# A two-layer DiT block on one core: four modulation groups summed row block by row block on VectorE, ScalarE and GpSimd instead of TensorE, layer 1's in layer 0's dense part

## The chip, the cores and the metric

The kernel runs on one core of a Trainium2 chip. Its engines are TensorE (PE; its weight loads are the rows PEld), VectorE (DVE), ScalarE (ACT), GpSimd (POOL) and SyncE (SP), which issues most of the transfers. The metric is the device time of one execution in microseconds (us), as the median of several.

## The reference

Two token streams, x and ctx, of 256 tokens by 1024 channels pass two layers; of layer 1 only x is needed. Cut to what matters:

```
mod_x = silu(c) @ w_mod[l] + b_mod[l]            # 1024 x 6144, six vectors
sh1, sc1, g1, sh2, sc2, g2 = split(mod_x, 6)     # and the same for ctx from c_ctx
p = modulate(rmsnorm(x, norm1_g[l]), sh1, sc1) @ w_in[l]
q, k, v, conv, pool, gate = split_in(p)
y = sigmoid(ga) * (attn @ w_attn_o) + sigmoid(gb) * (conv_module @ w_conv_o) + sigmoid(gc) * (pooled @ w_pool_o)
x = x + g1 * (y @ w_out[l])
x = x + g2 * expert_choice_ffn(modulate(rmsnorm(x, norm2_g[l]), sh2, sc2), ...)   # 16 experts, 12 MB each
```

So the modulation is a product of one or two vectors with a 1024 x 6144 matrix per layer. The kernel deals with it in three groups of 2048 columns: group 0 holds shift and scale of the first norm, group 1 the gate g1 and the shift of the second norm, group 2 its scale and the gate g2.

## The kernel before

**Units.** A layer's dense part works through products of the normalised tokens (512 columns in layer 0, 256 in layer 1) with weight blocks of 128 columns. Each such `unit` loads half of a 1 MB block (`w`, a ring of five buffers of 1 MB, filled by SP's queue in program order), splits it (`split`: ScalarE copies the high part, L227; VectorE or GpSimd, by the table `LOW`, subtracts for the low part, L228) and runs three passes of eight matmuls (`mm3`: L483, L484, and L486 with the low part). The units in order are q, k and v, the convolution's, the pooling's, and three merges (0, 2, 1) with eight gate units each. Each unit of a merge has an own output product beside it and ends on VectorE with `m` (L743, merge 0) or `th` (L746, the others), which in the latter case GpSimd adds to m (L748).

**Attention and convolution.** After a q or k product ScalarE reads it out (`raw`, L512, and `qx`, L529), GpSimd applies the rotary tables in two operations (L517 and L518), and ScalarE writes `QC` and `QS` (L535). v is turned by PE and copied to `vt` by VectorE (L556). The depthwise convolution of 31 taps runs on VectorE as multiply-adds (L465); they are issued a few at a time among the units (the table `TAPS`).

**Modulation.** `mod_group` forms one group on PE: for each of 8 blocks of 128 rows (a k-step), four matmuls (L244) whose stationary operand is silu(c), of 32 columns, and whose moving operand is the weight block of 128x2048 in four strips of 512. Bias, transposes and copies follow. It is a Python generator, and `pump_mod` advances it by one k-step per unit (every second unit in layer 1). Layer 0 so runs its own groups 1 and 2 and layer 1's group 0; layer 1 runs its groups 1 and 2. Layer 0's group 0 is formed ahead of all in another function, which stays.

**Order.** The program is put in order on each engine by a scheduler, with the program's order as priority; splits have a higher one (`SPLIT_PRIO`). `prefetch` asks for the first expert weights (`we`), in layer 0 two of them after attention. After the dense part come the product with w_out (L859), the routing, and 16 experts whose weights stream in blocks of 1 MB.

Of the kernel before, what the change touches and what calls it, by code (L numbers as in the profile page):

```python
# [10 lines left out]
F32 = mybir.dt.float32  # L11
F32R = mybir.dt.float32r
BF16 = mybir.dt.bfloat16
# [16 lines left out]
MOD_EVERY = (1, 2)  # L30
MOD_AHEAD = 1
# [3 lines left out]
KC_ID, KC_PERM, KC_IOTA, KC_SCOL, KC_EDGE, KV_C, KV_VEC, KV_END = 0, 128, 256, 288, 289, 353, 369, 433  # L35


def const_tables():

    f = np.float32  # L40
    kc = np.zeros((128, KV_C), f)
    p = np.arange(128)
    kc[:, KC_ID:KC_ID + 128] = np.eye(128, dtype=f)
    kc[p ^ 16, KC_PERM + p] = 1.0
    kc[:, KC_IOTA:KC_IOTA + 32] = np.arange(1, 33)
    kc[:, KC_SCOL] = p % 32 + 1
# [21 lines left out]
    return kc, b16.astype(mybir.dt.np(BF16)), rope.reshape(128, 2 * SEQ)  # L68


def laid_out(a):

    kc, b16, rope = const_tables()
    L = DEPTH
# [12 lines left out]
    cols = np.concatenate([dwc, snk], axis=2)  # L87
# [3 lines left out]
    bm[0, 0] = np.repeat(first, 32, axis=0)  # L91
    w_in = a["w_in"].reshape(L, 8, 128, 21, 256).transpose(0, 3, 2, 1, 4).copy()
# [3 lines left out]
    def blocks(w, order):  # L96
# [10 lines left out]
        ("w_mod0", w_mod0.reshape(2, 4, 128, 2048)), ("w_mod", a["w_mod"]), ("b_mod", bm),  # L107
# [13 lines left out]
def dit_block(ctx: ExitStack, tc: tile.TileContext, out, kcv, kb16, rope_in, tok, cols, w_mod0, w_mod,  # L121
# [53 lines left out]
    bt = P0.tile([128, 768], BF16, name="bt")  # L175
    identb, maskb = bt[:, 0:128], bt[:, 128:384].rearrange("p (a b) -> p a b", a=2)
    ucat = bt[:, 384:768].rearrange("p (a b) -> p a b", a=3)
# [4 lines left out]
    cst = P0.tile([128, 8, 2, 16], F32, name="cst")  # L182
# [18 lines left out]
    for l in range(DEPTH):  # L201
# [14 lines left out]
        nsplit, nunit, tail = [0], [0], [False]  # L216
# [14 lines left out]
        def mod_group(ll, g):  # L231
            ps = bank("md")

            def mload(k):
                return load(w_mod[ll, k * 128:(k + 1) * 128, g * 2048:(g + 1) * 2048], "p n -> p n")

            w = mload(0)
            for k in range(8):
                if k == 6:
                    bias = t2("modb", 512)  # L240
                    nc.scalar.dma_start(bias, b_mod[ll, g])
                wn = mload(k + 1) if k < 7 else None
# [18 lines left out]
            ptv = pt.rearrange("p (b j s m) -> p s j b m", b=4, j=4, s=2)
            for s in range(2):
                nc.vector.tensor_copy(modT[ll][:, g, s, :].rearrange("p (j b) -> p j b", j=4),
                                      ptv[:, s, :, :, 0])
            if g == 0:
                for s in range(2):
# [3 lines left out]
            if g == 2:  # L270
                for s in range(2):
# [15 lines left out]
        def layer_vectors():
            nc.scalar.dma_start(dws, cols[l])
# [3 lines left out]
        dws = DR.tile([128, 4 * CK + NH], F32, name="dw")  # L292
        dw, sink = dws[:, :4 * CK], dws[:, 4 * CK:]
# [126 lines left out]
        if l == 0:  # L420
# [5 lines left out]
            nc.scalar.dma_start(bt, kb16)  # L426
# [10 lines left out]
        wr = P0.tile([128, 8, 32], F32, tag="wr", name="wr")  # L437
        nc.scalar.dma_start(wr.rearrange("p k e -> p (k e)"), w_router[l])
        nc.sync.dma_start(rope.rearrange("p a t -> p (a t)"), rope_in)
        bg = deque([[(0, 1), (0, 2), (1, 0)], [(1, 1), (1, 2)]][l])  # L440
        cur_mod = [None]

        def pump_mod(n=1):

            while n > 0:
                if cur_mod[0] is None:
                    if not bg:
                        return
                    cur_mod[0] = mod_group(*bg.popleft())
                if next(cur_mod[0], "end") == "end":  # L450
                    cur_mod[0] = None
                else:
                    n -= 1
# [15 lines left out]
        if last:  # L469
            pump_mod(MOD_AHEAD)  # L470
# [17 lines left out]
        def unit(src, n, view="p (k n) -> p k n", eng="v", **kw):  # L488
# [21 lines left out]
        def roped(dst, ps):  # L510
# [3 lines left out]
            nc.tensor.matmul(pr[:, 0:256], kc[:, KC_PERM:KC_PERM + 128], raw, start=True, stop=True)  # L514
# [168 lines left out]
        prefetch(4 if last else 2)  # L683
# [6 lines left out]
        for u in range(2):  # L690
            wz = win(OP + 256 * u)
            for v in range(2):
# [19 lines left out]
                ed = kc[:, KC_EDGE + 16 * g:KC_EDGE + 16 * g + 16]  # L712
# [39 lines left out]

        merge(0, w_attn_o, br)
# [54 lines left out]
        pump_mod(100)  # L808
# [375 lines left out]
```

## Time and profile before

| | |
|---|---|
| median of 3 runs | 1722.48 us (1722.29 to 1725.2) |
| the profiled execution | 1721.98 us, span 1720.2 us |
| PE busy | 1515.4 us, 88% of the span |
| VectorE, ScalarE, GpSimd busy | 672.5, 407.7, 229.7 us |
| moved by DMA | 530 MB, mean 308 GB/s |

The rows below come from the profiled execution. Times are from the start of its span. A busy share over the whole span mixes dense parts and expert parts.

### The profile page before, as it was taken

The numbers are of one execution on the slowest core, as the hardware profiler recorded it, in microseconds if no ns is written. First come the engines' busy times: TensorE is split into PE (matmuls) and PEld (weight loads), VectorE is DVE, ScalarE is ACT, GpSimd is POOL, SyncE is SP. The second block draws the span as 40 slices with busy tenths as digits, with TensorE's granted clock in tenths as the row PEclk, the third lists the DMA queues.
The fourth block names the chain that finished last, engine by engine and source line by source line (L and its number), as shares of the span: only waits on it lengthen the run. The fifth ranks groups of instructions, "written<-read, shape, count | busy, mean of one in ns | idle before, by whom it ended". The sixth has DMA issues, their size and how long they took to land. (4 is left out here: it accounts for less than half of the span.)

```text
span 1720.2 us, 19498 instructions
## 1 busy us (share of the span) xinstructions
PE 1515.4 (88%) x7788; PEld 822.1 (48%) x7788; DVE 672.5 (39%) x1137; ACT 407.7 (24%) x760; POOL 229.7 (13%) x234
## 2 busy tenths in 40 slices
PE   6999989999999999999999899999979766666675
PEld 2665667888654433333333367789844111111111
DVE  3568993352552221221211368975532110111111
ACT  3455312232432100100000257334421000000001
POOL 0300520154640000000000020225100000000000
PEclk9999999999999999999999999999989898988989
DMA  9733445244536999999999864566789999999996
GB/s 398 276 122 129 147 147 202 78 152 165 220 147 267 421 421 421 421 420 421 421 422 420 334 240 178 201 232 226 278 334 420 421 421 421 421 421 421 422 421 272
DMA packets 78171, 530.04 MB, mean 308 GB/s; under 512 B 8449, under 2 KB 9217, under 8 KB 15106
## 3 DMA queue, kind: packets, MB, share of 16 engines
q1 hardware_dynamic: 76208, 526.12, 76.5%
q10 hardware_dynamic: 1874, 2.70, 0.5%
q8 instruction: 61, 1.00, 0.2%
q14 instruction: 28, 0.23, 0.0%
HBM read 527.73 MB, written 1.05 MB: 307 GB/s over the span
## 5 line engine op out<-in xcount | busy, mean ns | idle before, releaser
L1065 PE MATMUL mm<-we,xeT 128*64 128x512 f32 (+1 forms) x2048 | 414.4, 620 | 78.6 <-DMA we<-in_w_e_up_dram 59.7
L1065 PEld LDWEIGHTS mm<-we,xeT 128*64 128x64 f32 (+1 forms) x2048 | 125.0, 125 | 361.7 <-issue 191.5
L483 PE MATMUL mm<-hh,ws 128*128 128x512 f32 (+1 forms) x672 | 223.0, 350 | 0.2
L484 PE MATMUL mm<-hl,ws 128*128 128x512 f32 (+1 forms) x672 | 219.2, 345 | 0.8 <-DVE hl L418 0.8
L227 ACT ACTIVATE ws<-w 128x1024 fp32r<-128x1024 f32 x132 | 139.2, 1057 | 300.3 <-PE mm L486 196.9
L1072 DVE TENSOR_TENSOR hm<-si,mm 64x512 f32<-64x512 f32 x48 | 33.1, 690 | 419.7 <-ACT si L1070 283.1
L1070 ACT ACTIVATE si<-mm 64x512 f32<-64x512 f32 x48 | 28.4, 591 | 693.8 <-PE mm L1065 693.8
L465 DVE SCALAR_TENSOR_TENSOR acc<-up,dw,acc 128x512 f32<-128x512 f32 (+1 forms) x240 | 156.6, 692 | 1.1
L228 DVE TENSOR_TENSOR ws<-w,ws 128x1024 fp32r<-128x1024 f32 x94 | 124.7, 1329 | 67.5 <-ACT ws L227 67.4
L483 PEld LDWEIGHTS mm<-hh,ws 128*128 128x128 f32 x672 | 128.1, 191 | 28.8 <-issue 11.8
L484 PEld LDWEIGHTS mm<-hl,ws 128*128 128x128 f32 x672 | 128.1, 191 | 19.6 <-issue 3.5
L1088 PE MATMUL mm<-we,hT 128*64 128x512 f32 x512 | 126.1, 625 | 8.4 <-ACT hT L1083 8.4
L486 PE MATMUL mm<-hh,ws 128*128 128x512 f32 (+1 forms) x672 | 132.6, 339 | 0.7 <-DVE ws L228 0.6
L228 POOL TENSOR_TENSOR ws<-w,ws 128x1024 fp32r<-128x1024 f32 x38 | 95.4, 2517 | 213.9 <-ACT ws L227 213.9
L486 PEld LDWEIGHTS mm<-hh,ws 128*128 128x128 f32 x672 | 107.2, 189 | 15.3 <-DVE ws L228 1.3
L1030 POOL COPY sel<-kc 48x128 f32<-48x128 f32 (+1 forms) x16 | 4.6, 287 | 806.4 <-DVE hm L1072 434.6
L1093 PE MATMUL mm<-we,hT 128*32 128x512 f32 x512 | 83.4, 764 | 15.0 <-DMA we<-in_w_e_down_dram 11.2
L1100 DVE TENSOR_TENSOR Y<-mm,G 32x512 f32<-32x512 f32 x64 | 44.0, 687 | 126.4 <-PE mm L1088 125.7
L1088 PEld LDWEIGHTS mm<-we,hT 128*64 128x64 f32 x512 | 38.3, 143 | 86.3 <-issue 72.4
L1110 PE MATMUL ax<-Y,sg 128*128 128x512 f32 x128 | 62.5, 636 | 8.0 <-DVE Y L1103 6.4
L1080 PE MATMUL ax<-kc,hm 64*128 64x64 f32 x192 | 32.4, 291 | 31.1 <-DVE hm L1072 30.3
L1103 DVE TENSOR_TENSOR Y<-mm,G 64x512 f32<-64x512 f32 x32 | 22.0, 689 | 95.2 <-PE mm L1093 94.8
(254 smaller groups left out, 1624.3 us busy)
## 6 DMA issues: line engine op xcount, KB each, us to landing
we<-in_w_e_gate_dram SPq DMA_DIRECT2D x128, 1024.0 KB, 19.8
we<-in_w_e_up_dram SPq DMA_DIRECT2D x128, 1024.0 KB, 19.8
we<-in_w_e_down_dram SPq DMA_DIRECT2D x120, 1024.0 KB, 19.8
w<-in_w_mod_dram SPq DMA_DIRECT2D x44, 1024.0 KB, 6.3
w<-in_w_in_dram SPq DMA_DIRECT2D x42, 1024.0 KB, 4.9
w<-in_w_out_dram SPq DMA_DIRECT2D x12, 1024.0 KB, 4.8
we<-in_w_e_down_dram SPq DMA_DIRECT2D x16, 512.0 KB, 14.8
wm<-in_w_mod_dram SPq DMA_DIRECT2D x4, 1024.0 KB, 18.1
```

The costliest lines, as they stand in the source:

```text
L227: nc.scalar.activation(h, src, AF.Copy)
L228: (nc.gpsimd if eng == "p" else nc.vector).tensor_sub(lw, src, h.bitcast(F32))
L465: nc.vector.scalar_tensor_tensor(acc[:, ch], up[:, ch, :, k:k + 256], dw[:, 4 * k + ch:4 * k + ch + 1], acc[:, ch], op0=ALU.mult, op1=ALU.add)
L483: nc.tensor.matmul(ps, wh[:, k, :], ah[:, k, :n], start=k == 0, stop=False)
L484: nc.tensor.matmul(ps, wh[:, k, :], al[:, k, :n], start=False, stop=False)
L486: nc.tensor.matmul(ps, wl[:, k, :], ah[:, k, :n], start=False, stop=k == nk - 1)
L1065: nc.tensor.matmul(o, xeT[k // 4][:, k % 4, e, :], w[:, kk, 512 * f:512 * f + 512], start=k == 0, stop=k == 7)
L1072: nc.vector.tensor_mul(hm[0:64, :], si[0:64, :], pgu[f][64:128, :])
L1088: nc.tensor.matmul(pd[64 * h:64 * h + 64, :], hT[:, 64 * k:64 * k + 64], rhs, start=k == 0, stop=k == 7)
L1093: nc.tensor.matmul(pd[o:o + 32, :], hT[:, c0:c0 + 32], rhs, start=k < 2, stop=k >= 6)
L1100: nc.vector.tensor_mul(Y[b0:b0 + 32, s, cols], pd[rw, :], G2[l][rw, :])
L1110: nc.tensor.matmul(po, sgs[s][:, t * 128:(t + 1) * 128], Y[:, s, cols], start=True, stop=True)
```

## The change

A generator `vmod` takes the place of `mod_group`. It has three forms.

- Layer 1's group 0 stays on PE, with 256-column strips.
- Layer 0's groups 1 and 2 are summed on VectorE: each block of 128 rows and 1024 columns is multiplied by that block's column of silu(c) and added to an accumulator `macc` of 128x1024 per stream (L279 for the first block, L281 for the others; 64 in all).
- Layer 1's groups 1 and 2, of stream x only, are summed by two engines: ScalarE multiplies a block in place (L275, 32 in all) and GpSimd adds it to the accumulator (L277, 28).

For each half of a group one product of `macc` with a matrix of ones (L295, eight matmuls of 256 columns) then sums over the 128 partitions. There are two generators, `vgen`: PE's and VectorE's groups in the first, ScalarE's and GpSimd's in the second. `pump_mod` advances both after every unit, by the counts of `VSTEPS` for the stage. All of it, layer 1's w_mod loads too, is in layer 0's dense part; layer 1 keeps a selection and one matmul (`gate2`). The accumulators use the buffers in which the first two experts' weights were prefetched, so layer 0's prefetch moves behind merge 1. w_mod is laid out in blocks of 1 MB, the router's weights are loaded later, and some constant tables move to other buffers.

```diff
-MOD_EVERY = (1, 2)
-MOD_AHEAD = 1
+VSTEPS = dict(qkv=(1, 1), conv=(1, 1), pool=(2, 1), merge=(3, 1))
...
-        def mod_group(ll, g):
...
-                for j in range(4):
-                    nc.tensor.matmul(ps[32 * j:32 * j + 32, :],
-                                     cst[:, k].rearrange("p s m -> p (s m)"),
-                                     w[:, j * 512:(j + 1) * 512], start=k == 0, stop=k == 7)
-                w = wn
+        def vmod(ll, gs, tag):
+            pairs = [(gs[0], 0), (gs[0], 1)] if len(gs) == 1 else [(g, 0) for g in gs]
+            def mload(i):
+                hf, k2 = divmod(i, 4)
+                ws = [load(w_mod[ll, g, hf, k2], "p (k n) -> p k n", k=2) for g in gs]
+                return ws if len(gs) == 2 else ws * 2
...
+                for k2 in range(4):
+                    i = 4 * hf + k2
+                    wn = mload(i + 1) if i < 7 else None
+                    for kk in range(2):
+                        k = 2 * k2 + kk
...
+                        for q, (g, s) in enumerate(pairs):
+                            cs = csil[:, 8 * s + k:8 * s + k + 1]
+                            wk = w[q][:, kk]
+                            if len(gs) == 2:
+                                nc.scalar.activation(wk if k else ac[:, q], wk, AF.Copy, scale=cs)
+                                if k:
+                                    nc.gpsimd.tensor_add(ac[:, q], ac[:, q], wk)
+                            elif k == 0:
+                                nc.vector.tensor_scalar(ac[:, q], wk, cs, None, op0=ALU.mult)
+                            else:
+                                nc.vector.scalar_tensor_tensor(ac[:, q], wk, cs, ac[:, q],
+                                                               op0=ALU.mult, op1=ALU.add)
+                            yield
...
+                if tag is not None:
+                    for _ in range(3):
+                        yield
+                    ps = bank("md")
+                    for q in range(2):
+                        for j in range(4):
+                            nc.tensor.matmul(ps[32 * j:32 * j + 32, 0:256], ones[:, q],
+                                             ac[:, q, 256 * j:256 * j + 256], start=q == 0, stop=q == 1)
+                nc.vector.tensor_add(mr[:, 256 * hf:256 * hf + 256], ps[:, 0:256], bias)
...
-        bg = deque([[(0, 1), (0, 2), (1, 0)], [(1, 1), (1, 2)]][l])
...
+        vgen = [[], []]
+        if not last:
+            def on_dve():
+                yield from vmod(1, (0,), None)
+                yield from vmod(0, (1,), "e0")
+                yield from vmod(0, (2,), "e0")
+            vgen = [on_dve(), vmod(1, (1, 2), "e1")]
...
+            for g, n in zip(vgen, VSTEPS[vphase[0]] if every is None else (every, every)):
+                for _ in range(n):
+                    next(g, None)
...
-        prefetch(4 if last else 2)
+        if last:
+            prefetch(4)
...
         merge(1, w_conv_o, brc)
-        pump_mod(100)
+        pump_mod(1000)
+        if not last:
+            prefetch(2)
```

ScalarE's order before, from the read-out of the first q product on (names with buffer numbers; in the changed kernel L512, L529, L535 and L227 are L562, L579, L585 and L234):

```order
L512 ACTIVATE raw_353<-mm_318 128x256
L529 ACTIVATE qx_352<-mm_318 128x256
L535 ACTIVATE QC_313<-qx_352 64x256 x2
L535 ACTIVATE QS_310<-qx_352 64x256
L227 ACTIVATE ws_424<-w_422 128x1024
L227 ACTIVATE ws_476<-w_422 128x1024
L535 ACTIVATE QS_310<-qx_352 64x256
L512 ACTIVATE raw_405<-mm_373 128x256
L529 ACTIVATE qx_404<-mm_373 128x256
L535 ACTIVATE QC_313<-qx_404 64x256 x2
```

The same place after, from the read-out of the second q product on:

```order
L562 ACTIVATE raw_431<-mm_394 128x256
L275 ACTIVATE w_365<-w_365,csil_68 128x1024
L579 ACTIVATE qx_430<-mm_394 128x256
L275 ACTIVATE w_368<-w_368,csil_68 128x1024
L585 ACTIVATE QS_315<-qx_430 64x256
L585 ACTIVATE QC_318<-qx_430 64x256
L585 ACTIVATE QS_315<-qx_430 64x256
L585 ACTIVATE QC_318<-qx_430 64x256
L275 ACTIVATE w_368<-w_368,csil_68 128x1024
L275 ACTIVATE w_370<-w_370,csil_68 128x1024 x2
L234 ACTIVATE ws_450<-w_448 128x1024
L234 ACTIVATE ws_508<-w_448 128x1024
```

Seven L275 now stand behind the first read-out and ahead of the split of the next weight, L234 on w_448; five of them are in the rows above, and two stand before the rows' first, among the operations on the first product.

GpSimd's order there before, over the first q products:

```order
L517 TENSOR_TENSOR qx<-raw,rope 128x256
L518 TENSOR_TENSOR qx<-qx,rot 128x256
L517 TENSOR_TENSOR qx<-raw,rope 128x256
L518 TENSOR_TENSOR qx<-qx,rot 128x256
L517 TENSOR_TENSOR qx<-raw,rope 128x256
```

And after (L517 and L518 are now L567 and L568):

```order
L567 TENSOR_TENSOR qx<-raw,rope 128x256
L277 TENSOR_TENSOR macc<-macc,w 128x1024
L568 TENSOR_TENSOR qx<-qx,rot 128x256
L567 TENSOR_TENSOR qx<-raw,rope 128x256
L568 TENSOR_TENSOR qx<-qx,rot 128x256
L277 TENSOR_TENSOR macc<-macc,w 128x1024 x5
```

One L277 stands between the two rotary operations of the first product, and five stand ahead of the third product's.

VectorE's order in merge 0 before, from the third m on (L465 is the convolution, L228 the low part of a split):

```order
L743 SCALAR_TENSOR_TENSOR m<-th,mm 128x512
L465 SCALAR_TENSOR_TENSOR acc<-up,dw,acc 128x512 x4
L228 TENSOR_TENSOR ws<-w,ws 128x1024
L743 SCALAR_TENSOR_TENSOR m<-th,mm 128x512
L228 TENSOR_TENSOR ws<-w,ws 128x1024 x2
L743 SCALAR_TENSOR_TENSOR m<-th,mm 128x512
L228 TENSOR_TENSOR ws<-w,ws 128x1024
L743 SCALAR_TENSOR_TENSOR m<-th,mm 128x512
L228 TENSOR_TENSOR ws<-w,ws 128x1024 x2
L743 SCALAR_TENSOR_TENSOR m<-th,mm 128x512
```

And after (L801 is m, L519 the convolution, L235 the low part, L297 the addition of a bias), up to the fifth m:

```order
L235 TENSOR_TENSOR ws<-w,ws 128x1024
L297 TENSOR_TENSOR GM<-md,modb 128x256
L279 TENSOR_SCALAR macc<-w,csil 128x1024
L801 SCALAR_TENSOR_TENSOR m<-th,mm 128x512
L279 TENSOR_SCALAR macc<-w,csil 128x1024
L281 SCALAR_TENSOR_TENSOR macc<-w,csil,macc 128x1024 x6
L801 SCALAR_TENSOR_TENSOR m<-th,mm 128x512
L519 SCALAR_TENSOR_TENSOR acc<-up,dw,acc 128x512
L235 TENSOR_TENSOR ws<-w,ws 128x1024 x2
L281 SCALAR_TENSOR_TENSOR macc<-w,csil,macc 128x1024 x4
L235 TENSOR_TENSOR ws<-w,ws 128x1024
L801 SCALAR_TENSOR_TENSOR m<-th,mm 128x512
```

The multiply-adds of layer 0's group 1 (L279, L281) stand between the m, where before only low parts and a few convolution taps stood; taps from before the first m have moved in between too.

GpSimd's order there before, from the last pooling sums to merge 2's additions to m:

```order
L708 TENSOR_TENSOR zs<-zs 128x2x257
L715 TENSOR_TENSOR zs<-zs,kc 128x8 x4
L748 TENSOR_TENSOR m<-m,th 128x512 x5
L777 TENSOR_SCALAR rl<-bmv 128x1
L778 TENSOR_TENSOR rl<-rl,nhalf 128x1
```

And after (L806 is the addition to m):

```order
L773 TENSOR_TENSOR zs<-zs,dw 128x8 x4
L277 TENSOR_TENSOR macc<-macc,w 128x1024 x10
L806 TENSOR_TENSOR m<-m,th 128x512
L277 TENSOR_TENSOR macc<-macc,w 128x1024 x2
L806 TENSOR_TENSOR m<-m,th 128x512
L277 TENSOR_TENSOR macc<-macc,w 128x1024 x2
L806 TENSOR_TENSOR m<-m,th 128x512 x3
```

Ten L277 stand between the last pooling operation and merge 2's first addition, and four more among the next two.

## Rows read from the trace of the kernel before

**Rows 1.** The page: busy times; DMA share in 40 slices of 43 us, tenths.

```profile
PE 1515.4 (88%) x7788; PEld 822.1 (48%) x7788; DVE 672.5 (39%) x1137; ACT 407.7 (24%) x760; POOL 229.7 (13%) x234
...
DMA  9733445244536999999999864566789999999996
```

**Rows 2.** Windows: layer 0's dense part; stretch, length, busy us (instructions) by engine.

```profile
47.00:82.00 35.00, 34.75 (x167) 23.66 (x165) 20.40 (x29) 17.49 (x35) 13.23 (x12) 1.00 0.71 261
...
82.00:235.70 153.70, 145.78 (x662) 93.26 (x661) 130.11 (x228) 67.37 (x155) 37.13 (x42) 0.98 0.37 128
...
235.70:297.70 62.00, 62.00 (x292) 44.67 (x292) 33.59 (x43) 14.11 (x18) 0.00 (x0) 1.00 0.60 211
...
297.70:362.30 64.60, 64.60 (x297) 52.61 (x296) 34.74 (x46) 20.11 (x26) 15.99 (x18) 1.00 0.25 88
...
362.30:437.70 75.40, 75.40 (x331) 61.77 (x330) 20.49 (x20) 23.35 (x32) 36.51 (x22) 1.00 0.46 169
```

**Rows 3.** VectorE's timeline in merges 0 and 1: start us, us, instruction, [idle before <-releaser].

```profile
278.88 0.69 DVE L743 SCALAR_TENSOR_TENSOR m<-th,mm 128x512 f32<-128x512 f32 x1 [1.71 <-PE mm L486]
...
288.26 0.69 DVE L743 SCALAR_TENSOR_TENSOR m<-th,mm 128x512 f32<-128x512 f32 x1 [1.70 <-PE mm L486]
...
378.65 0.69 DVE L746 SCALAR_TENSOR_TENSOR th<-th,mm 128x512 f32<-128x512 f32 x1 [1.75 <-issue]
...
386.81 0.69 DVE L746 SCALAR_TENSOR_TENSOR th<-th,mm 128x512 f32<-128x512 f32 x1 [7.47 <-PE mm L486]
```

**Rows 4.** By form (ns min/median/max, first and last start); one row of VectorE's timeline.

```profile
L465 DVE SCALAR_TENSOR_TENSOR acc<-up,dw,acc x240: 454/736/2891, 102.2 to 1145.5; 128x512 f32<-128x512 f32 x60, 128x256 f32<-128x256 f32 x60
...
L227 ACT ACTIVATE ws<-w x132: 1037/1059/1087, 22.9 to 1244.9; 128x1024 fp32r<-128x1024 f32 x132
...
L228 POOL TENSOR_TENSOR ws<-w,ws x38: 2375/2404/3146, 63.4 to 1176.8; 128x1024 fp32r<-128x1024 f32 x38
...
183.42 6.70 DVE L465 SCALAR_TENSOR_TENSOR acc<-up,dw,acc 128x512 f32<-128x512 f32 x10
```

**Rows 5.** Timeline of VectorE and GpSimd in two stretches, both busy.

```profile
438.24 11.39 DVE L814 TENSOR_TENSOR ml<-m,mh 128x512 fp32r<-128x512 f32 x6
...
440.04 8.45 POOL L228 TENSOR_TENSOR ws<-w,ws 128x1024 fp32r<-128x1024 f32 x3
...
192.48 6.37 DVE L465 SCALAR_TENSOR_TENSOR acc<-up,dw,acc 128x512 f32<-128x512 f32 x5
...
194.04 2.76 POOL L228 TENSOR_TENSOR ws<-w,ws 128x1024 fp32r<-128x1024 f32 x1 [9.77 <-ACT ws L227]
```

**Rows 6.** Timeline after the first q product, and the start of attention.

```profile
47.61 0.38 ACT L512 ACTIVATE raw<-mm 128x256 f32<-128x256 f32 x1 [5.14 <-PE mm L486]
...
49.35 0.91 POOL L518 TENSOR_TENSOR qx<-qx,rot 128x256 f32<-128x256 f32 x1 [0.55 <-DVE rot L516]
...
50.61 1.99 ACT L227 ACTIVATE ws<-w 128x1024 fp32r<-128x1024 f32 x2
...
51.70 0.19 PEld L483 LDWEIGHTS mm<-hh,ws 128*128 128x128 f32 x1 [1.03 <-ACT ws L227]
...
82.23 0.69 DVE L556 COPY vt<-ax 128x512 f32<-128x512 f32 x1 [0.24 <-PE ax L555]
```

**Rows 7.** Layer 1: first and last of seven L244 pieces of the chain; windows.

```profile
1036.79 0.99 PE md L244 x6
...
1175.54 1.00 PE md L244 x8
...
980.00:1000.00 20.00, 17.21 (x93) 10.04 (x92) 16.83 (x31) 13.25 (x31) 3.51 (x5) 1.00 0.45 172
...
1100.00:1120.00 20.00, 17.40 (x140) 15.10 (x138) 19.91 (x43) 5.84 (x8) 4.60 (x7) 1.00 0.70 257
```

**Rows 8.** The expert parts: last pieces of the chain; a window of layer 0.

```profile
1655.13 19.85 DMA we<-in_w_e_down_dram
...
550.00:600.00 50.00, 49.31 (x260) 22.44 (x258) 12.00 (x21) 7.61 (x15) 0.58 (x2) 1.00 1.01 416
```

More of the change, by code (lines that the diff above doesn't have):

```diff
@@ L67, in const_tables @@
     b16[:, 640:768] = 1.0
-    return kc, b16.astype(mybir.dt.np(BF16)), rope.reshape(128, 2 * SEQ)
+    return kc, dk, b16.astype(mybir.dt.np(BF16)), rope.reshape(128, 2 * SEQ)
 def laid_out(a):
-    kc, b16, rope = const_tables()
+    kc, dk, b16, rope = const_tables()
     L = DEPTH
@@ L91, in laid_out @@
     bm[0, 0] = np.repeat(first, 32, axis=0)
+    bm[1, 1] = np.where(np.arange(128)[:, None] % 32 < 16, bm[1, 1], bm[1, 2])
+    w_mod = a["w_mod"].reshape(L, 4, 2, 128, 3, 4, 2, 256).transpose(0, 4, 6, 1, 3, 2, 5, 7)
     w_in = a["w_in"].reshape(L, 8, 128, 21, 256).transpose(0, 3, 2, 1, 4).copy()
@@ L174, in dit_block @@
         nc.sync.dma_start(XS[s].rearrange("p t d -> p (t d)"), tok[s])
-    bt = P0.tile([128, 768], BF16, name="bt")
-    identb, maskb = bt[:, 0:128], bt[:, 128:384].rearrange("p (a b) -> p a b", a=2)
-    ucat = bt[:, 384:768].rearrange("p (a b) -> p a b", a=3)
+    bt = P0.tile([128, 384], BF16, name="bt")
+    ucat = bt.rearrange("p (a b) -> p a b", a=3)
+    ones = P0.tile([128, 2, 32], F32, name="ones")
+    for i in range(2):
+        for j in range(2):
+            nc.vector.memset(ones[:, i, 16 * j:16 * j + 16], float(i == j))
     nc.scalar.activation(csil, ccol, AF.Tanh, scale=0.5)
@@ L265, in mod_group @@
-            if g == 0:
-                for s in range(2):
+                                      ptv[:, q, :, :, 0])
+                if g == 0:
                     nc.vector.scalar_tensor_tensor(
@@ L269, in mod_group @@
                         vec[:, VN1 + 8 * ll:VN1 + 8 * ll + 8], op0=ALU.add, op1=ALU.mult)
-            if g == 2:
-                for s in range(2):
+                if g == 2:
                     nc.vector.scalar_tensor_tensor(
@@ L436, in dit_block, with pump_mod @@
             qw = [qload(0)]
-        wr = P0.tile([128, 8, 32], F32, tag="wr", name="wr")
-        nc.scalar.dma_start(wr.rearrange("p k e -> p (k e)"), w_router[l])
+            layer_tables()
         nc.sync.dma_start(rope.rearrange("p a t -> p (a t)"), rope_in)
-        bg = deque([[(0, 1), (0, 2), (1, 0)], [(1, 1), (1, 2)]][l])
[L441 to L453, printed above, removed]
+        vgen = [[], []]
[5 more added lines that the diff above has]
+            vgen = [on_dve(), vmod(1, (1, 2), "e1")]
+        vgen = [iter(v) for v in vgen]
+        vphase = ["qkv"]
+        def pump_mod(every=None):
+            for g, n in zip(vgen, VSTEPS[vphase[0]] if every is None else (every, every)):
+                for _ in range(n):
+                    next(g, None)
         taps = deque()
@@ L513, in roped @@
             pr = bank("ax")
-            nc.tensor.matmul(pr[:, 0:256], kc[:, KC_PERM:KC_PERM + 128], raw, start=True, stop=True)
+            nc.tensor.matmul(pr[:, 0:256], perm, raw, start=True, stop=True)
             rot = t2("rot", 256)
@@ L681, in dit_block @@
             pass
-        prefetch(4 if last else 2)
+        if last:
+            prefetch(4)
+        vphase[0] = "pool"
         wp = DR.tile([128, 4, 128], F32, tag="k2", name="wp")
@@ L751, in merge @@
                         next(fill, None)
+        vphase[0] = "merge"
         merge(0, w_attn_o, br)
```

112 lines of the change are left out of this document (64 added, 48 removed).

## The prediction

> **What bounds the kernel now.** The page's first lines come first. TensorE is busy for 1515.4 of 1720.2 us, but the line of DMA shares shows two regimes: long runs of 9, where the experts' weights stream, and 300 to 450 us ahead of each, the dense part of a layer, with shares of mostly .2 to .7 [rows 1]. So the dense parts must be read by themselves.
>
> The second view cuts layer 0's dense part into five stages [rows 2]: the q, k and v units (47 to 82 us), attention, convolution and pooling (82 to 235.7), seven units of merge 0 (to 297.7), seven of merge 2 (to 362.3), the rest of it and merge 1 (to 437.7). PE is full in the three merge stages and idle for 0.25 us in the first. Only in the second it isn't: 145.8 of 153.7 us, with VectorE at 130.1, the busiest there after PE. In the merges VectorE works for 33.6 of 62, 34.7 of 64.6 and 20.5 of 75.4 us, and GpSimd for 0, 16.0 and 36.5.
>
> The third view is VectorE's timeline in merge 0: the unit that ends with an m comes every 9.38 us, and VectorE has waited 1.7 us for PE before it; later, with no modulation step in the unit, th follows th after 8.16 us and the wait is 7.5 us [rows 3]. The difference fits the step, eight matmuls of which take 1.0 us [rows 7].
>
> Layer 1's dense part alternates: a PE step of the modulation stands on the chain of waits between 1036 and 1176 us seven times; between 1100 and 1120 VectorE is busy for 19.9 of 20 us and PE for 17.4, so PE's load doesn't count there [rows 7]. From about 1290 on, the chain is one transfer of 1 MB after another, 19.8 us each, and in layer 0 the share is 1.01 from 550 us on [rows 8]. A dense part that ends later or earlier therefore moves the whole expert part behind it, one for one.
>
> **The change, part by part.** It takes two of layer 0's three groups and two of layer 1's off PE: 16 k-steps in layer 0 and 16 in layer 1. In their place VectorE gets 64 operations on 128x1024 (8 first products, 56 multiply-adds), ScalarE 32 and GpSimd 28, all in layer 0's dense part.
>
> *Their price.* A multiply-add on 512 columns takes 0.74 us, the shortest (256 columns) 0.45; 0.27 to 0.29 per 256 columns more gives 1.28 us for 1024 (estimate), so 64 are at most 82 us of VectorE. ScalarE's pass over 1024 columns takes 1.06 us: 34 us. GpSimd's only operation of that size, the low part of a split, takes 2.40 us: 28 are 67 us [rows 4]. Those are durations without company. In company, rows show more: six ml subtractions on VectorE take 11.39 us while GpSimd does three subtractions in 8.45 instead of 7.2; five multiply-adds, 0.67 each in a run of ten [rows 4], take 6.37 us, 3.0 too long, when one GpSimd subtraction of 2.76 falls among them [rows 5]. The two engines take turns, operation by operation, when both read two operands from SBUF.
> The Trainium skill states this (SBUF — State Buffer, section "SBUF: two separate sides"): the pair of ports that both engines use is an exclusive lock, held for the whole instruction, for a VectorE operation with two SBUF inputs against a GpSimd operation that reads SBUF. The rows agree (2.76 of GpSimd, 3.0 lost on VectorE), and the rule speaks against giving sums to both at once. Without it the merges' term below would be 4 instead of 28.
>
> *The start.* In the row of before, ScalarE reads out a q unit (L512, 47.61), and 3 us later splits the next weight (L227, 50.61), after which PE goes on at 51.70; POOL's two rope operations end at 50.26 [rows 6]. In the new order seven L275 stand between that read-out and the split, 7 x 1.06 = 7.4 us, and one L277 stands between the two rope operations, 2.4 us more, for whose result ScalarE's QS waits. PE has nothing else than modulation steps there: +10. The next weight loads stand behind w_mod loads in SP's queue, some of which wait for GpSimd's L277 to free a buffer; five L277 more stand ahead of the third q rope, and four ahead of k's, 2.4 each. Before, PE was full up to v, whose copy vt starts at 82.23 [rows 2, 6], so every wait counts until attention starts. Part of these hides behind the units themselves; I take +15 in all (bounds +10, as the chain of ScalarE alone; +20, if four of the nine L277 are seen in full).
>
> *Attention to pooling.* VectorE decides there. By the order, 37 of its multiply-adds of the convolution come after the first m instead of before (37 x 0.70 = 26 us less), and 14 L281 and two L279 come in (16 x 1.28 = 20 us more), which leaves about -6; five PE steps of 1.0 us fewer stand there, and PE has 8 us idle in all. I take -8 (bounds -11 and -2).
>
> *Merge 0.* By the order the same seven units hold 38 instead of 23 multiply-adds of the convolution (+15 x 0.70 = 10.5) and 16 new operations (14 x 1.28 + 2 x 0.75 = 19.5): VectorE's 33.6 become about 64 [rows 2]. Ten L277 of GpSimd fall in it, where there was nothing: 24 us. PE without its steps would need about 7 x 8.3 = 58. If the two engines didn't disturb each other VectorE would set 64 (+2); if all of it took turns, 88 (+26). Eight of VectorE's operations read PSUM and (m, at 0.69 in [rows 3]) and should not take turns, and some of GpSimd's fall where VectorE waits for ScalarE's half of a split; I take 80: +18.
>
> *Merge 2.* 22 multiply-adds moved there (15 us), 13 L281 and two L279 (18 us): VectorE's 34.7 become 67. GpSimd's 16.0 become 25.6 with four L277. Alone, VectorE would be 2 beyond the 64.6; in turns 93, +28. Here more of the work on both sides is from PSUM or waits on PE (the convolution's norm), so I take 75: +10. *Merge 1* has VectorE at 20.5 plus the rest of the L281, about 43 of 75 us, with GpSimd at 36.5: 80 in turns at worst, +1 (0 to +5). The last product, two small ones per half and transposes instead of 8 k-steps, is PE's: some 6 us for six halves against 16 us saved, and counts only where PE sets the pace, which it then does not.
>
> *Layer 1.* 16 k-steps of 1.0 us, minus those where VectorE or another wait sets the pace: seven on the chain (7 us) and five or six of the nine between 980 and 1030, where PE is busy for 17 of 20 us [rows 7]: -13 (bounds -9 and -18). Experts' weights asked for after merge 1 instead of after attention have room in the shares of .5, .3 and .6 of the slices from 430 us to 550 [rows 1]: 0 (to +3).
>
> *Sum:* +15 - 8 + 18 + 10 + 1 - 13 = +23. The profiled execution took 1721.98 us (1720.2 of span), 0.5 below the median of 1722.48. So 1721.98 + 23 = 1745.
>
> **The rivals.** *VectorE has the room (faster).* In the merges VectorE is idle for 113 of 202 us [rows 2]; if its sums and GpSimd's fall into that, PE stays the bound and the merges shrink: 16 k-steps less, 6 us of products more, -10 in layer 0, -13 in layer 1, the start's stall +10 partly regained in attention (-8): about -20, 1702. For it: VectorE alone comes out at 64 and 67, no more than 2 beyond the stages' present length. Against it: that is already no room at all, and the turns of [rows 5]. It decides where VectorE and GpSimd together stay below 8.3 us per unit; by the sums they need up to 12.6.
> *All in turns, loads late (slower still).* With the serial sums, 88 and 93, and the upper start, the terms are +20 - 2 + 26 + 28 + 5 - 9 = +68; half way from the forecast, about +45, 1767. For it: w_in loads now stand in SP's queue behind loads that wait for GpSimd to finish. Against: of GpSimd's work something always falls where VectorE waits.
> *It nets out (same).* Merges at 66 to 70 each (+8), start +10, attention -8, layer 1 -13: -3 to 0. It needs GpSimd's adds to land in VectorE's waits for ScalarE by half.
>
> **How the numbers follow.** About 0.2% (3.4 us) is what a measurement of this kernel tells from no change. Chances: forecast of +8 to +40 0.58; all in turns 0.18; netted out 0.08; room 0.16. Slower by over 0.2%: 0.76; the same 0.08; faster 0.16. The likeliest case by itself spans 1730 to 1762. For 8 in 10 the range takes in the serial sum's half and the upper part of the faster rival: 1714 to 1770.
>
> **What the changed profile would show.** ScalarE: seven L275 between the first q read-out and the next split, PE's next unit near 62 instead of 51.7 us, vt near 97 instead of 82. VectorE: L281 above 1.28 us in the mean, with single ones of 3 to 3.6 beside an L277. m in merge 0 every 11 us or more, with PE idle before a low-part matmul and released by VectorE's split; merge 1 at 8 to 8.5 per unit. Layer 1's dense part about 13 us shorter, the expert parts of unchanged length. The prediction is wrong if merge 0's units stay at or under 9.4 us, if the start costs nothing (PE covers it with other units), or if L277 and L281 run side by side at their own durations.

## The result, and the profile after

The changed kernel takes 1761.74 us (median of 4; 1760.4 to 1765.65), the kernel before 1722.38 on the same chip: a ratio of 1.0229, with an interval of 1.0208 to 1.025, or 39 us more. The profiled execution is the longest of the four, 1765.65 us with a span of 1763.9, 43.7 beyond the span of before; the stages below add up to that.

The page's busy times, TensorE's granted clock and the DMA shares after:

```profile
PE 1510.9 (86%) x7688; PEld 833.9 (47%) x7688; DVE 788.2 (45%) x1207; ACT 440.1 (25%) x792; POOL 322.4 (18%) x262
...
PEclk9899998999999999999999989999989989898898
...
DMA  9653225354574899999999963344679999999996
```

VectorE and GpSimd have 116 and 93 us more than in [rows 1]; PE has 4.5 less. The five stages of layer 0's dense part, cut at the same events as [rows 2] (start, vt, first m, last m, seventh th, last th), in the same columns (stretch, its length, then busy us and number of instructions of PE, of its weight loads, of VectorE, ScalarE and GpSimd, then TensorE's granted clock as a share of 2.4 GHz, the DMA share and GB/s):

```profile
47.00:99.00 52.00, 37.70 (x185) 26.34 (x183) 27.90 (x29) 28.66 (x46) 36.64 (x22) 0.84 0.62 232
...
99.00:248.70 149.70, 136.85 (x615) 93.77 (x614) 123.43 (x205) 73.18 (x161) 45.91 (x42) 0.95 0.32 116
...
248.70:329.20 80.50, 66.00 (x280) 49.49 (x279) 80.50 (x75) 25.09 (x28) 30.25 (x10) 0.89 0.57 211
...
329.20:410.60 81.40, 69.29 (x322) 55.32 (x320) 79.06 (x85) 23.14 (x30) 35.42 (x22) 0.98 0.37 131
...
410.60:492.30 81.70, 79.03 (x374) 61.32 (x374) 51.64 (x52) 25.31 (x35) 43.16 (x25) 1.00 0.56 195
```

In merge 0 VectorE is busy for all of 80.5 us and PE for 66.0, in merge 2 for 79.1 of 81.4 and PE for 69.3: the engine that sets the pace has changed. The granted clock is 0.84 in the first stage and 0.89 in merge 0, where PE has begun to wait. The start on the timeline, which answers to [rows 6]:

```profile
46.99 0.38 ACT L562 ACTIVATE raw<-mm 128x256 f32<-128x256 f32 x1 [3.60 <-PE mm L538]
...
48.49 2.39 POOL L277 TENSOR_TENSOR macc<-macc,w 128x1024 f32<-128x1024 f32 x1 [0.29 <-ACT w L275]
...
55.61 12.40 POOL L277 TENSOR_TENSOR macc<-macc,w 128x1024 f32<-128x1024 f32 x5
...
57.17 3.23 ACT L275 ACTIVATE w<-w,csil 128x1024 f32<-128x1024 f32 x3
...
58.17 2.57 DVE L586 TENSOR_TENSOR QC<-qx,QC 64x256 fp32r<-64x256 f32 x1
...
60.30 1.99 ACT L234 ACTIVATE ws<-w 128x1024 fp32r<-128x1024 f32 x2
...
61.40 0.29 PEld L535 LDWEIGHTS mm<-hh,ws 128*128 128x128 f32 x1 [4.51 <-ACT ws L234]
...
99.23 0.69 DVE L606 COPY vt<-ax 128x512 f32<-128x512 f32 x1
```

Between the read-out of the first q product and the next split (60.30) lie the L275, and GpSimd's five L277 from 55.61 on; PE goes on at 61.40 instead of 51.70, and vt comes at 99.23 instead of 82.23. VectorE's passes over QC and QS (L586) fall beside those additions and take 2.5 to 2.6 us each, where one without company takes 0.42 (no_sums, below). PE is busy for only 3.8 of the 10 us from 52 to 62, and from 57 to 67 its granted clock is 0.51, the lower of its two levels (1.2 of 2.4 GHz).

Two m of merge 0, 8.4 us apart:

```profile
278.93 0.67 DVE L801 SCALAR_TENSOR_TENSOR m<-th,mm 128x512 f32<-128x512 f32 x1
...
287.36 0.68 DVE L801 SCALAR_TENSOR_TENSOR m<-th,mm 128x512 f32<-128x512 f32 x1
```

These are close together, against [rows 3]; but between the first and the last m lie 80.5 us, 11.5 per unit. What fills the others is in merge 0's groups (busy us, mean ns | idle before, released by):

```profile
L519 DVE SCALAR_TENSOR_TENSOR acc<-up,dw,acc 128x512 f32<-128x512 f32 x39 | 43.2, 1158 | 0.0
...
L281 DVE SCALAR_TENSOR_TENSOR macc<-w,csil,macc 128x1024 f32<-128x1024 f32 x14 | 17.1, 1274 | 0.0
...
L235 DVE TENSOR_TENSOR ws<-w,ws 128x1024 fp32r<-128x1024 f32 x10 | 14.2, 1433 | 0.0
...
L277 POOL TENSOR_TENSOR macc<-macc,w 128x1024 f32<-128x1024 f32 x10 | 30.3, 3037 | 42.6 <-ACT w L275 30.1 <-ACT macc L275 12.1
...
L538 PEld LDWEIGHTS mm<-hh,ws 128*128 128x128 f32 x56 | 12.5, 227 | 16.8 <-DVE ws L235 14.1
```

A multiply-add of the convolution (L519) takes 1158 ns in the mean instead of some 740, a low part (L235) 1433 instead of 1220; L281 is not stretched here at all, at 1274: thirteen of its fourteen stand where GpSimd makes no addition. One in merge 2 that has an addition beside it, at 357.36 us, takes 3.42. PE's weight load for the low part (L538) has waited 16.8 us, 14.1 of them for VectorE's L235. Single rows show how it comes about:

```profile
255.90 5.20 POOL L277 TENSOR_TENSOR macc<-macc,w 128x1024 f32<-128x1024 f32 x2 [12.12 <-ACT macc L275]
...
256.07 5.58 DVE L519 SCALAR_TENSOR_TENSOR acc<-up,dw,acc 128x512 f32<-128x512 f32 x2
...
280.19 7.26 DVE L281 SCALAR_TENSOR_TENSOR macc<-w,csil,macc 128x1024 f32<-128x1024 f32 x6
```

Two multiply-adds take 5.58 us while GpSimd makes two additions in 5.20; six L281 without an addition beside them take 7.26, 1.21 each. Layer 1, from vt to the last output of the merges (window of before, then of after):

```profile
1028.30:1226.30 198.00, 192.58 (x1425) 162.94 (x1425) 148.44 (x278) 97.62 (x172) 54.29 (x64) 0.99 0.57 204
```

```profile
1081.60:1267.00 185.40, 177.96 (x1322) 159.28 (x1321) 146.44 (x269) 97.13 (x172) 58.12 (x60) 0.99 0.42 149
```

198.0 us have become 185.4.

### The profile page after: what moved, and what is told of

Its sections match the earlier page's. It is cut to its first block, busy times and chain, and to the rows that moved or that the text cites. A ratio compares the mean times of both kernels' runs of the same rounds, so it can differ in the third digit from the quotient of the medians.

```text
span 1763.9 us, 19476 instructions
## 1 busy us (share of the span) xinstructions
PE 1510.9 (86%) x7688; PEld 833.9 (47%) x7688; DVE 788.2 (45%) x1207; ACT 440.1 (25%) x792; POOL 322.4 (18%) x262
## 5 line engine op out<-in xcount | busy, mean ns | idle before, releaser
L535 PE MATMUL mm<-hh,ws 128*128 128x512 f32 (+1 forms) x672 | 226.1, 356 | 7.2 <-ACT ws L234 5.7
L536 PE MATMUL mm<-hl,ws 128*128 128x512 f32 (+1 forms) x672 | 223.8, 352 | 0.8 <-DVE hl L471 0.8
L234 ACT ACTIVATE ws<-w 128x1024 fp32r<-128x1024 f32 x132 | 139.2, 1057 | 260.1 <-PE mm L538 155.4
L519 DVE SCALAR_TENSOR_TENSOR acc<-up,dw,acc 128x512 f32<-128x512 f32 (+1 forms) x240 | 175.0, 770 | 1.0
L538 PE MATMUL mm<-hh,ws 128*128 128x512 f32 (+1 forms) x672 | 139.7, 349 | 20.8 <-DVE ws L235 18.2
L535 PEld LDWEIGHTS mm<-hh,ws 128*128 128x128 f32 x672 | 131.1, 196 | 28.3 <-ACT ws L234 9.0
L235 DVE TENSOR_TENSOR ws<-w,ws 128x1024 fp32r<-128x1024 f32 x94 | 128.0, 1365 | 35.3 <-ACT ws L234 35.0
L1149 PE MATMUL mm<-we,hT 128*64 128x512 f32 x512 | 130.5, 640 | 8.4 <-ACT hT L1144 8.4
L235 POOL TENSOR_TENSOR ws<-w,ws 128x1024 fp32r<-128x1024 f32 x38 | 102.2, 2693 | 149.2 <-ACT ws L234 147.6
L538 PEld LDWEIGHTS mm<-hh,ws 128*128 128x128 f32 x672 | 109.5, 193 | 38.6 <-DVE ws L235 20.8
L277 POOL TENSOR_TENSOR macc<-macc,w 128x1024 f32<-128x1024 f32 x28 | 76.4, 2738 | 75.1 <-ACT w L275 62.3
L281 DVE SCALAR_TENSOR_TENSOR macc<-w,csil,macc 128x1024 f32<-128x1024 f32 x56 | 78.9, 1441 | 0.0
```

The source lines that it names most:

```text
L234: nc.scalar.activation(h, src, AF.Copy)
L235: (nc.gpsimd if eng == "p" else nc.vector).tensor_sub(lw, src, h.bitcast(F32))
L277: nc.gpsimd.tensor_add(ac[:, q], ac[:, q], wk)
L281: nc.vector.scalar_tensor_tensor(ac[:, q], wk, cs, ac[:, q], op0=ALU.mult, op1=ALU.add)
L519: nc.vector.scalar_tensor_tensor(acc[:, ch], up[:, ch, :, k:k + 256], dw[:, 4 * k + ch:4 * k + ch + 1], acc[:, ch], op0=ALU.mult, op1=ALU.add)
L535: nc.tensor.matmul(ps, wh[:, k, :], ah[:, k, :n], start=k == 0, stop=False)
```

## The experiments

All ratios are to the kernel before on the same chip. The stages of each run's profile, in us, are cut as above; the last column is layer 1 from vt to the last mh (ScalarE's high part of the merged stream).

| run | time, ratio [interval] | to vt | to first m | merge 0 | merge 2 | to last th | layer 1 |
|---|---|---|---|---|---|---|---|
| before | 1722.4 | 82.2 | 153.5 | 61.9 | 64.7 | 75.3 | 198.0 |
| changed | 1761.7, 1.0229 | 99.2 | 149.5 | 80.5 | 81.4 | 81.7 | 185.4 |
| no_adds | 1721.5, 0.9995 [0.9984, 1.0006] | 93.8 | 142.5 | 59.2 | 73.6 | 81.6 | 185.5 |
| no_dve_sums | 1748.8, 1.0154 [1.0133, 1.0175] | 99.0 | 151.7 | 71.9 | 71.2 | 81.2 | 185.6 |
| no_sums | 1717.7, 0.9968 [0.9956, 0.998] | 92.8 | 147.5 | 59.4 | 65.1 | 81.2 | 185.5 |
| adds_on_vector | 1744.9, 1.0126 [1.0109, 1.0144] | 95.6 | 147.2 | 65.4 | 87.1 | 81.3 | 185.9 |
| later_start | 1745.4, 1.0144 [1.0126, 1.0161] | 80.8 | 170.8 | 74.7 | 74.6 | 80.0 | 185.6 |
| layer0_part | 1723.3, 1.0002 [0.9989, 1.0015] | 80.9 | 141.1 | 57.6 | 76.8 | 78.8 | 202.3 |
| layer1_part | 1758.8, 1.0217 [1.0192, 1.0241] | 99.1 | 165.3 | 76.8 | 66.3 | 76.7 | 185.7 |
| fills_for_adds | 1722.9, 1.0000 [0.9988, 1.0012] | 92.3 | 143.1 | 61.2 | 72.5 | 83.3 | 185.4 |
| loads_only | 1707.8, 0.9909 [0.9896, 0.9922] | 84.0 | 148.7 | 59.4 | 65.1 | 81.1 | 185.5 |
| layer1_on_vector | 1714.9, 0.9963 [0.995, 0.9976] | 80.7 | 150.5 | 68.3 | 68.1 | 76.1 | 185.6 |
| layer1_on_vector_late | 1724.3, 1.0001 [0.9989, 1.0013] | 80.8 | 150.5 | 62.3 | 78.2 | 76.3 | 185.4 |

**Which sums cost what: four runs.** The first, no_adds:

```diff
                                 nc.scalar.activation(wk if k else ac[:, q], wk, AF.Copy, scale=cs)
-                                if k:
-                                    nc.gpsimd.tensor_add(ac[:, q], ac[:, q], wk)
```

> Leaves out GpSimd's 28 additions L277 (layer 1's groups 1 and 2 are then not summed); ScalarE's 32 passes, all loads and VectorE's 64 operations stay. Theory A, VectorE and GpSimd take turns, so that the two sums cost more together than apart: the merges fall from 244 us (first m to last th in the changed kernel) to VectorE's own 64 and 67 and PE's 76, about 207, and the start gives back some 7 of its 17; about 1762 - 37 - 7 = 1718. Theory B, the loads of w_mod, late or in the way in SP's queue: they are all still there, so it stays above 1745. Theory C, VectorE's own added work alone: only the start gives back, about 1755.

It came to 1721.5 us: 40 us back, as theory A had it. By stages it differs: merge 0 is even 59.2, with VectorE busy for all of it and PE for 58.3, but merge 2 is 73.6 and not 67, and the last stage 81.6 and not 76. Theories B and C fall, since all loads and all of VectorE's sums are still there.

The second, no_dve_sums:

```diff
-                            else:
-                                nc.vector.scalar_tensor_tensor(ac[:, q], wk, cs, ac[:, q],
-                                                               op0=ALU.mult, op1=ALU.add)
```

> Leaves out VectorE's 56 multiply-adds L281 (layer 0's groups 1 and 2 are then not summed; the 8 first products stay); GpSimd's additions, ScalarE's passes and all loads stay. Theory A: in merge 0 VectorE has 46 and GpSimd 24 us, in merge 2 50 and 26, which mostly fit under PE's 58 to 60 with some turns lost: merges at 66, 68 and 76 instead of 244 in all, -34, the start unchanged at +17: about 1728. Theory B (loads): above 1745. A theory D, that GpSimd's additions alone do it: above 1745 too, with the merges hardly shorter than in the changed kernel.

1748.8, not 1728: theory A's number missed by 20, and D's time came true. D's other half did not: merges 0 and 2 are 71.9 and 71.2 instead of 80.5 and 81.4, so VectorE's sums have a part there. The window of its merge 0, and the convolution in this run (L516) and in the run without any sums (L514, no_sums below):

```profile
250.70:322.60 71.90, 62.30 (x277) 48.18 (x276) 58.03 (x58) 24.44 (x28) 27.20 (x10) 0.93 0.62 236
...
L516 DVE SCALAR_TENSOR_TENSOR acc<-up,dw,acc 128x512 f32<-128x512 f32 x36 | 40.2, 1151 | 0.5
...
L514 DVE SCALAR_TENSOR_TENSOR acc<-up,dw,acc 128x512 f32<-128x512 f32 x36 | 25.7, 751 | 0.5
```

VectorE 58.0 and PE 62.3 of 71.9, GpSimd 27.2. In no_sums VectorE's work of that stage, the same 36 multiply-adds, 11 low parts and small ones, is 43.3; the 14.7 us that it has more here are nearly all the convolution's (40.2 instead of 25.7), work that it always had. So the additions need no new partner to cost.

The third, no_sums, is both edits together:

> Leaves out both GpSimd's L277 and VectorE's L281; ScalarE's passes, the 8 first products, the products with ones and all loads stay. Theory A: the merges go to PE's pace without modulation steps (8.2 per unit): 58, 60, 76, so 8 below the kernel before; attention some 5 to 8 shorter; the start +8 for ScalarE's passes; layer 1 -12: about 1705 (1698 to 1712). If both apart give back 44 and 34 and together less than their sum, they took turns: the time that needs both engines is what is counted twice. Theory B (loads): most of the 39 us stays, above 1745.

1717.7, 13 above what was expected: the start kept 10.6 us instead of 8, merge 2 took 65.1 instead of 60, and the last stage 81.2 instead of 76, of which more below. With it the four times can be read as a square: VectorE's sums alone add 3.8 us (1721.5), GpSimd's additions alone 31.1 (1748.8), both 44.0 (1761.7). Only 9 are due to the two meeting.

The fourth, adds_on_vector:

```diff
-                                    nc.gpsimd.tensor_add(ac[:, q], ac[:, q], wk)
+                                    nc.vector.tensor_add(ac[:, q], ac[:, q], wk)
```

> The 28 additions on VectorE instead of GpSimd; everything is still computed. Theory A: 28 x 1.25 = 35 us more on VectorE, 67 less on GpSimd. Merge 0: 64 + 10 x 1.25 = 76; merge 2 67 + 5 = 72, with GpSimd's own 16 some 76; merge 1 76; 228 instead of 244. At the start VectorE has room, about -6. Attention and pooling about +3. About 1762 - 16 - 6 + 3 = 1743. Theory D, GpSimd's pace sets when buffers come free for SP's loads: more than 30 comes back, under 1732.

1744.9. The total is as expected, the stages aren't: merge 0 has 65.4 and merge 2 87.1. VectorE with all sums still does better than VectorE and GpSimd together, by 17 us.

**Turns or occupation: fills_for_adds.**

```diff
-                                    nc.gpsimd.tensor_add(ac[:, q], ac[:, q], wk)
+                                    nc.gpsimd.memset(wk, 0.0)
+                                    nc.gpsimd.memset(wk, 0.0)
```

> In place of each of GpSimd's 28 additions stand two fills of the same weight buffer with zeros, which wait for the same ScalarE pass, free the buffer at their end, and read nothing from SBUF; layer 1's groups 1 and 2 are then not summed. Two fills should keep GpSimd busy for about as long as one addition. If the merges grew because the two engines take turns at operands read from SBUF, they come out as in the run without additions, 59, 74 and 82 us, and the whole at 1722 to 1730 (the start keeps its +17). If GpSimd's occupation or the late release of buffers did it, the merges stay at 80, 81 and 82 and the whole above 1750.

1722.9, with merges of 61.2, 72.5 and 83.3. Merge 0's groups in this run (L520 is the convolution, L282 the sums):

```profile
L520 DVE SCALAR_TENSOR_TENSOR acc<-up,dw,acc 128x512 f32<-128x512 f32 x38 | 26.2, 751 | 0.0
...
L282 DVE SCALAR_TENSOR_TENSOR macc<-w,csil,macc 128x1024 f32<-128x1024 f32 x14 | 17.1, 1279 | 0.0
...
L235 DVE TENSOR_TENSOR ws<-w,ws 128x1024 fp32r<-128x1024 f32 x10 | 12.1, 1222 | 0.0
...
L278 POOL MEMSET w<- 128x1024 f32 x8 | 8.9, 1114 | 0.3
...
L277 POOL MEMSET w<- 128x1024 f32 x8 | 7.6, 957 | 38.2 <-ACT w L275 38.2
```

These are the operations of the changed kernel's merge 0 (38 instead of 39, 14 and 10), at 751, 1279 and 1222 ns; GpSimd was busy there for 16.5 us with fills that wait for the same passes and free the same buffers. Two fills are 1.9 us, an addition 2.4 to 2.6, so the match is not exact, but the stretch is gone altogether: 39 x 0.41 and 10 x 0.21 us, 18 of the 19.3 by which merge 0 is shorter than in the changed kernel. So VectorE's two-operand work takes turns with a GpSimd operation that reads its operands from SBUF; GpSimd's being busy, or the time at which it frees buffers, is not the cause in the merges. The Trainium skill (SBUF — State Buffer, section "SBUF: two separate sides") has just this condition, a VectorE operation with two SBUF inputs against a GpSimd operation that reads SBUF; the two runs agree with it.

The start did not keep its +17: vt comes at 92.3, as without additions, although GpSimd makes 20 fills (18.9 us) where it made ten additions (24.2 us). So the additions' part of the start, too, is not explained by their places in GpSimd's queue alone; VectorE's passes over QC and QS take 0.61 and 0.42 us in the mean there, against 1.34 and 0.89 in the changed kernel.

**The start: loads_only and later_start.** The first is no_sums without ScalarE's passes:

```diff
-                                nc.scalar.activation(wk if k else ac[:, q], wk, AF.Copy, scale=cs)
+                                if k == 0:
+                                    nc.scalar.activation(ac[:, q], wk, AF.Copy, scale=cs)
```

> The run without sums, and besides without ScalarE's 28 passes after the first of each accumulator: layer 1's loads of w_mod are all there, with hardly any work on them. The start of that run was 10.6 us later than before (vt at 92.8). If ScalarE's passes ahead of the next split are the cause, vt now comes at 82 to 85 us and the whole at 1707 to 1711; if the loads ahead of the next w_in in SP's queue are, vt stays at 90 to 93 and the whole near 1718.

vt comes at 84.0 and the whole takes 1707.8: of the start's 17 us, 8.8 are ScalarE's passes (92.8 to 84.0), 5 to 6 GpSimd's additions (99.2 against 93.8, 99.0 against 92.8 without them), and 1.8 is left for the loads and the rest. Part of the 8.8 is PE's clock after its waits: from 57 to 67 us the granted clock is 0.66 in no_sums and 1.00 in loads_only. It is also what the change could give at most if the sums and passes were free: 15 us.

```diff
-VSTEPS = dict(qkv=(1, 1), conv=(1, 1), pool=(2, 1), merge=(3, 1))
+VSTEPS = dict(qkv=(1, 0), conv=(1, 1), pool=(2, 3), merge=(3, 1))
```

> ScalarE's and GpSimd's generator stands still during the q, k and v units and catches up in the pooling units; everything is computed. If ScalarE's passes and GpSimd's additions between the q operations are the start's cost, vt comes at 82 to 84 us instead of 99. The 14 additions then fall in attention and convolution, where VectorE is the busiest: by the turns some 10 to 20 of that are lost again, so 1750 to 1762. If instead the 17 us are the price of loads that stand in SP's queue, they come back wherever the loads go; if turns cost nothing there, 1745.

1745.4, 16 less than the changed kernel, 5 better than the range that was given for turns. It is the very number that was named for turns that cost nothing, but by chance: the stages show that they cost. The start's delay is gone (80.8); 20 additions, not 14, now lie between vt and the first m, and that stage is 21 us longer. Its groups:

```profile
L519 DVE SCALAR_TENSOR_TENSOR acc<-up,dw,acc 128x512 f32<-128x512 f32 x61 | 69.4, 1170 | 0.1
...
L281 DVE SCALAR_TENSOR_TENSOR macc<-w,csil,macc 128x1024 f32<-128x1024 f32 x14 | 23.9, 1727 | 0.0
...
L277 POOL TENSOR_TENSOR macc<-macc,w 128x1024 f32<-128x1024 f32 x20 | 53.0, 2660 | 58.4 <-ACT w L275 58.2
```

The convolution is at 1170 ns, L281 at 1727: what was won at the start is lost in turns here. Merges 0 and 2, with fewer additions, gave back 13.

**One part alone: layer0_part, layer1_part.** In the first, layer 1's groups are PE's again, in layer 1; in the second, layer 0's are PE's (in both the steps per unit were set anew for PE, and some small tiles were moved to other buffers). The lines that matter, the first two of layer0_part, the rest of layer1_part:

```diff
-            vgen = [on_dve(), vmod(1, (1, 2), "e1")]
+            vgen = [on_dve(), []]
...
+                yield from vmod(0, (1,), None)
+                yield from vmod(0, (2,), None)
                 yield from vmod(1, (0,), None)
-                yield from vmod(0, (1,), "e0")
-                yield from vmod(0, (2,), "e0")
```

> Only VectorE's part of the change: layer 0's groups 1 and 2 on VectorE; layer 1's groups 1 and 2 on PE in layer 1 again. Start as before, +1; attention 143 to 146 instead of 153.5; merges as in the run without additions, 59 and 74; the rest 77 to 80; layer 1 as before: 1722 - 9 - 2 + 9 + 3 = 1723 (1716 to 1728). If VectorE's work by itself were the trouble, 1740 or more.

1723.3: VectorE's part by itself changes nothing in the whole. Layer 0's dense part ends 2.5 us earlier (435.1 us), layer 1 takes 4.3 longer than before.

> Only ScalarE's and GpSimd's part: layer 1's groups 1 and 2 by them in layer 0; layer 0's groups on PE as before. Start +17; attention 153; merge 0 and 2 as in the run without VectorE's sums, 72 and 71, or a little more for PE's steps; the rest 81; layer 1 -12: 1722 + 17 + 10 + 7 + 6 - 12 = 1750 (1743 to 1757). If GpSimd's additions cost only together with VectorE's new sums, 1728 or less.

1758.8, 2 above the range: ScalarE's and GpSimd's part is nearly all of the loss. Its merge 0 holds only 15 multiply-adds of the convolution, at 1286 ns, and still takes 76.8. That is not turns alone: PE is busy for 71.7 of it, partly with products that the kernel before has in other stages.

**A version that beats both: layer1_on_vector.** Layer 0's groups on PE, layer 1's on VectorE by L279 and L281's form, for x only, from the pooling units on (layer 0's groups as in layer1_part):

```diff
-                            if len(gs) == 2:
-                                nc.scalar.activation(wk if k else ac[:, q], wk, AF.Copy, scale=cs)
-                                if k:
-                                    nc.gpsimd.tensor_add(ac[:, q], ac[:, q], wk)
-                            elif k == 0:
+                            if k == 0:
...
+VSTEPS = dict(qkv=(1, 0), conv=(1, 0), pool=(1, 1), merge=(1, 2))
```

> Layer 0's groups on PE as before; layer 1's groups 1 and 2, of x alone, on VectorE in layer 0 (28 multiply-adds and 4 first products, from pooling on), without ScalarE and GpSimd. If VectorE's room in the merges holds such sums as long as GpSimd keeps out: start as before, attention +2 to +5, merges 64, 67 and 78, layer 1 -12: 1722 + 4 + 2 + 2 + 3 - 12 = 1721 (1712 to 1726). If VectorE's sums in the merges cost as in the changed kernel, above 1735.

1714.9, and repeated beside the next variant:

> The same kernel as the run with layer 1's groups on VectorE, beside the later variant on one chip: 0.996 of the kernel before, as there (0.995 to 0.998), if that gain is real.

1715.4, 0.9959 [0.9944, 0.9974]: 8 us faster than the kernel before. Its two merge stages:

```profile
231.20:299.50 68.30, 67.62 (x355) 50.12 (x354) 52.04 (x72) 13.67 (x18) 0.00 (x0) 1.00 0.64 236
...
299.50:367.60 68.10, 68.10 (x360) 53.61 (x359) 56.32 (x65) 20.71 (x27) 18.78 (x18) 1.00 0.74 281
```

PE is full again (67.6 of 68.3 and 68.1 of 68.1) beside 52 and 56 us of VectorE. These stages are still 6.4 and 3.4 us longer than before; the gain is layer 1's 12.4 us.

> As layer 1's groups on VectorE alone, but one step per unit in merge 0 and two only in merges 2 and 1, where VectorE has most room. Merge 0 was 6.4 us longer than before there, merge 2 3.4, the rest 0.8. Moving eight operations of 1.3 us to the last stage should give back 3 to 5: about 1711 (1708 to 1715). If VectorE's place in the merges doesn't matter, 1715.

1724.3: a miss. Merge 0 gave back 6 us, but merge 2 took 10 more, and 3 more were lost between the dense part and layer 1. Most of the shift between the merges is work of PE that moved across the cut, for it is busy for 135.0 us of both together here and for 135.7 there. What is lost in them is 4 us, PE's idle time of 5.5 instead of 0.7: 3.5 of it stands behind one low part that comes after a run of sums on VectorE. The 3 us behind the dense part are open.

## Why the prediction was right, and where it was off

It said slower, 1745, and it is 1761.7, inside the range, at the upper end of what its likeliest case spans (1730 to 1762). No errors cancelled: every term came out longer than forecast, most of all merge 2, the last stage and attention. Term by term, in the profiled execution:

- *Start, +15:* +17.0. Right, and from what it named, ScalarE's passes (8.8, at 1.14 us each and not 1.06) and GpSimd's additions (5 to 6); loads were nearly nothing. That the additions cost there by turns with VectorE too is what fills_for_adds suggests; PE's lower clock after its waits was in no term.
- *Attention to pooling, -8:* -4.0, inside its bounds. Four additions fall in that stage, and the term allowed nothing for turns with them; in no_adds it is -11.0.
- *Merge 0, +18:* +18.6. The sum of VectorE's 64 and GpSimd's 24, a little short of the serial 88, was the right picture; the turns are shown by fills_for_adds. But the partner was not the one that its signs put first: in this stage not the new L281, which kept 1274 ns because the order left it hardly an addition beside it, but the convolution and the low parts that had been there all along.
- *Merge 2, +10:* +16.7. The step that was off is the allowance for work that reads PSUM or waits on PE: 81.4 of a serial 93 were reached, not 75. Without additions VectorE's sums alone still make it 73.6, 6 above the 67 worked out.
- *The last stage, +1:* +6.4. The step that failed is that products and transposes count only where PE sets the pace, "which it then does not". Here it does. In the run without sums:

```profile
364.70:445.90 81.20, 81.20 (x389) 64.24 (x389) 29.23 (x36) 25.35 (x35) 37.80 (x26) 1.00 0.50 181
```

PE is full for 81.2 us against 75.4 in [rows 2], and the work that is new there is the modulation's end: three of the six products with ones (L290 in that run, L295 in the changed kernel), the selection for the gate (L325) and the transposes (L301). The first row is the changed kernel's, the others that run's:

```profile
L295 PE MATMUL md<-macc,ones 128*32 128x256 f32 x48 | 3.2, 385 | 0.0
...
L325 PE MATMUL ax<-vmr,gsel 128*128 128x512 f32 x2 | 1.0, 594 | 0.0
L301 PE MATMUL ax<-kc,vmr 128*128 128x128 f32 x4 | 0.9, 304 | 0.0
L301 PE MATMUL ax<-kc,GM 128*128 128x128 f32 x4 | 0.6, 280 | 0.0
```

That is 3.2 + 1.0 + 1.5 = 5.7 of the 5.8 us; before, the last k-step was done in an earlier stage.
- *Layer 1, -13:* -12.6, and it is the same in every run that freed layer 1 of its steps.

The stages of layer 0 are 54.7 us, where +36 was forecast; with -12.6 for layer 1 and +1.6 elsewhere that is the 43.7 of the profiled span. The rival in which all of it goes in turns named 1767, nearer to the result than the forecast, and was nearer in merge 2; the late loads that it added had next to no part in it (at most the 1.8 us left at the start). The rival in which VectorE has the room was wrong for this change, since GpSimd shares it, and half right for VectorE alone: layer1_on_vector, with 32 operations on VectorE, is that rival without GpSimd and gains 8 us, but layer0_part, with 64 and layer 1's groups on PE, gains nothing.

## What to carry to other kernels

Before work is shared out to an idle GpSimd, look at what VectorE does in the same stretch: if both read operands from SBUF, count much of GpSimd's time as added to VectorE's, however idle either looks by its share. Here 28 additions, 67 us of GpSimd at 2.4 each, cost 40 us there (31 without VectorE's new sums), and 23 on VectorE. A step in an in-order queue between a product's read-out and the next operand costs most of its length where PE has no other unit to do: the start's ten passes, 11.0 us of ScalarE in no_sums, cost 8.8, PE's clock included.

## What was not expected of the hardware

A fill of 128x1024 by GpSimd takes 0.95 us and, unlike an addition (2.35 us at least, 2.56 in the median), leaves VectorE's two-operand work at its own durations.
